# The sample's projections leave PSUM by two ScalarE copies and are summed in SBUF; the gated values are scaled in the order of their groups

## The chip, the core and the metric

The kernel runs on one core of one Trainium2 chip. The metric is the device time of one execution in microseconds (us). A core has five engines that run side by side, each through its own queue in order: PE (TensorE: matrix products and transposes; its weight loads are shown apart, as PEld), DVE (VectorE), ACT (ScalarE), POOL (GpSimd) and SP (SyncE, which here starts transfers). PE writes its results to PSUM, which this kernel handles as eight banks of 128 x 512 numbers; everything else lies in SBUF. An instruction that needs another engine's result, or a buffer that another engine still reads, waits at the head of its queue, and everything behind it waits too.

## What is computed

The program runs two layers of an encoder over 512 prompt positions and 32 sample positions, 544 together, of width 1024. A layer has a mixer, a cross-attention into 256 memory rows, and a feed-forward part with a short convolution. The change lies in the mixer, which in the reference is:

```
h = rmsnorm(x, w['norm_mix_g'])
z = h @ w['w_in']
q, k, v, u, gv = jnp.split(z, [c1, c2, c3, c4], axis=-1)
o = diff_attention(q, k_all, v_all, pos, k_pos, lam)
u = jax.nn.gelu(u)
gv = rmsnorm(jax.nn.gelu(gv).reshape(B, S, GM_GROUPS, GM_CH), w['gm_norm_g'])
g_out = spatial_gate(u, gv, w['gm_w_s'], w['gm_b'])
x = x + jnp.concatenate([o, g_out], axis=-1) @ w['w_out']
```

q, k and v feed a differential attention with four heads: two softmax maps per head, the second subtracted with a learned factor. u and gv feed a gate with four groups of 128 channels: each group of gv is normalized, multiplied by a lower triangular 128 x 128 matrix over chunks of 128 positions, and multiplied into u. Prompt and sample share the weights; the sample also attends to cached keys and values.

## The kernel before

**Precision.** A float32 operand is split into a high part and a low rest, and a product takes three matmuls: high by high, high by low, low by high. Weights arrive by DMA as `raw`, ACT casts the high part (L192) and DVE subtracts to get the rest (L193); both go to slots named `hl`, of which there are eight. These splits run ahead of their use in the gaps of ACT and DVE.

**Projections by position.** `proj_tm` (L374) makes a slice of 256 columns of k and q, of v or of gv. The prompt takes four groups of 24 matmuls (`tm_group`, L370 to L372) into two banks `pr`. The sample takes 16 matmuls (L387) into one bank `prs`: `xsm` holds the high and the low part of the sample's rows side by side, so that rows 0 to 31 of the bank hold the high part's product and rows 32 to 63 the low part's. `sum_s` (L409) adds the two: ACT copies rows 32 to 63 to a scratch (`zs1`, which the trace names `skq` after its tile), and DVE adds rows 0 to 31 of the bank and the scratch into `zs`, in a tile that the trace names `zvs`. It runs eight times a layer: four times for k and q, twice for v, twice for gv.

**Attention.** For a head, `kq_T` transposes k and q (`ptr`, and `ptrs` for the sample). `do_attn` then goes over four blocks of 128 queries: scores (L639, L641) into two banks `pS`; the maximum on DVE (L597), the exponential on ACT (L598), the two maps joined on DVE (L603); the result transposed on PE (L649, `paT`), copied by ACT (L651), and multiplied with v (L654, `po`); `take_o` copies it and sums its squares on ACT. After four blocks a chain of small DVE operations finds the scales (`subnorm`), ACT applies them (L624), PE transposes (L660, `poT`), and ACT and DVE put the head's output into `og`. `do_attn_sample` does the same for the 32 sample queries (`pSs`, `paTs`, `pos`, and `posT` for two heads together).

**Gate.** `do_gv` (L721) projects gv for two groups, applies the gelu in three DVE passes and two ACT passes, sums the squares of its eight 128 x 128 pieces (four chunks of two groups), finds the scales by a chain of small DVE operations (L744, then `rsq`: L247 to L254), and scales the eight pieces on ACT (L747). `do_us` projects u (L353 into `pua` and `pub`, 96 matmuls for a column of 128). `do_gate` (L754) multiplies four pieces of one group with its matrix (L763, `pg`) and then those of the other; DVE reads the result (L765) and multiplies it into u (L792). Then w_out is projected from `og` (L353, `pwoa` and `pwob`).

**What sets the order.** The layer's code fixes the heads, but the order in each engine's queue is made at build time by a scheduler that works with its own estimate of durations. PSUM comes from three pools: four banks "R" (`pr`, `prs`, `ptr`, `ptrs`, `pg`, `pgs`, `pua`, `pub`), two "S" (`pS`, `pSs`), two "B" (`paT`, `po`, `poT`, `paTs`, `pos`, `posT`). A bank goes to its next user when its last reader is done. So a small edit moves instructions far from its place.

Of the kernel before, what the change touches and what calls it, by code (L numbers as in the profile page):

```python
# [13 lines left out]
ALU = mybir.AluOpType  # L14
# [22 lines left out]
def encoder_step(ctx: ExitStack, tc: tile.TileContext, a, o):  # L37
    nc = tc.nc
    vec, act, pool, pe, sp = nc.vector, nc.scalar, nc.gpsimd, nc.tensor, nc.sync
# [10 lines left out]
    def psS(name):  # L50
        return pp.tile([128, 512], F32, tag="S", bufs=2, name=name)
# [6 lines left out]
    def G(tag, shape, name, dt=F32):  # L58
        return gp.tile(shape, dt, tag=tag, bufs=GB[tag], name=name)
# [6 lines left out]
    def tiny(shape, name, dt=F32):  # L66
        return tp.tile(shape, dt, tag="y_" + name, bufs=1 if name in ONCE else 2, name=name)
# [159 lines left out]
    def pop(tag, n=2):  # L227

        for i in state.pop("done", ()):
            state["held"] -= cost(i)  # L230
        i = state["popped"]
        prefetch()
        res = []
        for j in range(i, i + n):
            assert items[j][0] == tag, (items[j], tag)
            res.append(wt.pop(j))
        state["popped"] = i + n
        state["done"] = range(i, i + n)
        return res


    def rsq(v, p, n, name, eng=vec):

        y, h, t = (tp.tile([128, n], F32, tag=f"{name}_{v}", bufs=2 if v == "y" else 1, name=name + v)
                   for v in "yht")
        yy, hh, tt = y[0:p, 0:n], h[0:p, 0:n], t[0:p, 0:n]
        eng.tensor_scalar(out=yy.bitcast(I32), in0=v.bitcast(I32), scalar1=-0.5, scalar2=1597463007.0,  # L247
                          op0=ALU.mult, op1=ALU.add)
        eng.tensor_scalar(out=hh, in0=v, scalar1=-0.5, scalar2=None, op0=ALU.mult)
        for _ in range(3):  # L250
            eng.tensor_tensor(out=tt, in0=yy, in1=yy, op=ALU.mult)
            eng.tensor_tensor(out=tt, in0=tt, in1=hh, op=ALU.mult)
            if eng is vec:
                vec.scalar_tensor_tensor(out=yy, in0=tt, scalar=1.5, in1=yy, op0=ALU.add, op1=ALU.mult)  # L254
            else:
                eng.tensor_scalar(out=tt, in0=tt, scalar1=1.5, scalar2=None, op0=ALU.add)
                eng.tensor_tensor(out=yy, in0=tt, in1=yy, op=ALU.mult)
        return y
# [5 lines left out]
    def gelu2(z, t):  # L264

        act.activation(out=t, in_=z, func=AF.Square, scale=math.sqrt(0.044715))
        vec.scalar_tensor_tensor(out=t, in0=t, scalar=1.0, in1=z, op0=ALU.add, op1=ALU.mult)
        act.activation(out=t, in_=t, func=AF.Tanh, scale=GC)
        vec.scalar_tensor_tensor(out=z, in0=t, scalar=1.0, in1=z, op0=ALU.add, op1=ALU.mult)
# [32 lines left out]
    def psR2(name, n=0):  # L302
        f = psS if n % 3 == 2 else psR
        return [f(name + "a"), f(name + "b")]
# [69 lines left out]
    def proj_tm(w2):  # L374
        pr, pv = [], []
        for t in range(4):
            t0 = 128 * t
            if t % 2 == 0:
                ps = psR("pr").rearrange("p (t c) -> p t c", t=2)
            pr.append(ps[:, t % 2])  # L380
            tm_group(pr[t], lambda k: hx[:, k, 0, t0:t0 + 128], lambda k: hx[:, k, 1, t0:t0 + 128], w2)
            if t % 2:
                pv.append(ps)
        ps = psR("prs")
        for k in range(8):
            for part in range(2):
                pe.matmul(out=ps[0:64, 0:256], lhsT=xsm[:, k], rhs=w2[k // 4][part][:, k % 4],  # L387
                          start=(k == 0 and part == 0), stop=(k == 7 and part == 1))
        return pr, pv, ps
# [15 lines left out]
    def small_z(kind):  # L405
        small[kind].reverse()
        return small[kind][0]

    def sum_s(ps, name):  # L409
        zt = small["zs1"]  # L410
        zs = small_z("vs" if name == "vs" else "zs")
        act.copy(zt, ps[32:64, 0:256])
        vec.tensor_tensor(out=zs[0:32], in0=ps[0:32, 0:256], in1=zt, op=ALU.add)  # L413
        return zs


# [101 lines left out]
    def do_kq(l, h, ve):  # L518
        c = LC[l]
        pr, pv, prs = proj_tm(pop(f"kq{h}"))  # L520
        z = G("zr", [128, 4, 256], "z")
        sq = G("t4", [128, 4, 256], "sq")
        for i in range(2):
            act.copy(z[:, 2 * i:2 * i + 2], pv[i])
            act.activation(out=sq[:, 2 * i:2 * i + 2], in_=pv[i], func=AF.Square)
        zs = sum_s(prs, "zs")
        sqs = small["zs1"]
        act.activation(out=sqs, in_=zs[0:32], func=AF.Square)
        ss = tiny([128, 20], "ss")
        pool.memset(ss[:, 16:20], 1.0)  # L530
        vec.tensor_reduce(out=ss[:, 0:16], in_=sq.rearrange("p t (m d) -> p (t m) d", d=64), axis=AX, op=ALU.add)
        vec.tensor_reduce(out=ss[0:32, 16:20], in_=sqs.rearrange("p (m d) -> p m d", d=64), axis=AX, op=ALU.add)
        s5 = ss.rearrange("p (t m) -> p t m", m=4)
        vec.scalar_tensor_tensor(out=s5, in0=s5, scalar=1.0 / 64, in1=ve.unsqueeze(2).to_broadcast([128, 5, 4]),
                                 op0=ALU.mult, op1=ALU.add)
        rs = rsq(ss, 128, 20, "rk")
        norm_rope(z, 128, 4, None, rs[:, 0:16], c, 0)
        norm_rope(zs[0:32].unsqueeze(1), 32, 1, None, rs[0:32, 16:20], c, 4)
        sp.dma_start(out=o["dkp"][l, 0, :, h].rearrange("(t p) m d -> p t (m d)", p=128), in_=z[:, :, 0:128])
        sp.dma_start(out=o["dks"][l, 0, :, h].rearrange("p m d -> p (m d)"), in_=zs[0:32, 0:128])  # L540
        return z, zs
# [179 lines left out]
    def do_gv(l, j, r):  # L721
        c = LC[l]
        pr, _, prs = proj_tm(pop(f"gv{j}"))
        z = G("zr", [128, 4, 256], "gz")
        t1 = G("t4", [128, 4, 256], "gt")
        for t in range(4):
            act.activation(out=z[:, t], in_=pr[t], func=AF.Copy,
                           scale=r[:, t:t + 1])
        zs = sum_s(prs, "gzs")
        vec.tensor_scalar(out=zs[0:32], in0=zs[0:32], scalar1=r[0:32, 4:5], scalar2=None, op0=ALU.mult)  # L730
        t1s = small["zs1"]
        ss = tiny([128, 10], "gss")
        pool.memset(ss[:, 8:10], 1.0)
        gelu2(z, t1)
        gelu2(zs[0:32], t1s)
        z8 = z.rearrange("p t (g c) -> p (t g) c", c=128)
        zs2 = zs[0:32].rearrange("p (g c) -> p g c", c=128)
        for b in range(8):
            act.activation(out=t1[:, b // 2, 128 * (b % 2):128 * (b % 2) + 128], in_=z8[:, b], func=AF.Square,
                           accum_out=ss[:, b:b + 1])  # L740
        for b in range(2):
            act.activation(out=t1s[:, 128 * b:128 * b + 128], in_=zs2[:, b], func=AF.Square,
                           accum_out=ss[0:32, 8 + b:9 + b])
        vec.tensor_scalar(out=ss, in0=ss, scalar1=1.0 / 128, scalar2=4 * EPS, op0=ALU.mult, op1=ALU.add)  # L744
        rs = rsq(ss, 128, 10, "rg")
        for b in range(8):
            act.activation(out=z8[:, b], in_=z8[:, b], func=AF.Copy, scale=rs[:, b:b + 1])  # L747
        vec.tensor_tensor(out=zs2, in0=zs2, in1=rs[0:32, 8:10].unsqueeze(2).to_broadcast([32, 2, 128]), op=ALU.mult)
        vec.tensor_tensor(out=t1s.rearrange("p (g c) -> p g c", c=128), in0=zs2,
                          in1=c["gmg"][0:32].unsqueeze(1).to_broadcast([32, 2, 128]), op=ALU.mult)  # L750
        sp.dma_start(out=o["gvs"][l, 0, :, 2 * j:2 * j + 2].rearrange("p g c -> p (g c)"), in_=t1s)
        return z, zs
# [428 lines left out]
    for t in range(4):  # L1181
        for hk in range(2):
            ps = (psB if hk else psS)("pxin")
# [4 lines left out]
        if t == 0:  # L1188
            ps = psS("pxis")
# [11 lines left out]
    for l in range(DEPTH):  # L1201
# [25 lines left out]
        do_attn_sample_end(l, 0, og, st)  # L1227
        zk[3] = do_kq(l, 3, ve)
        vns[0] = do_gv(l, 0, r)
        kqs[3] = kq_T(l, 3, *zk[3])  # L1230
        do_attn(l, 3, kqs[3], vv[3], og)
        do_attn_sample(l, 3, kqs[3], vv[3], st)
        og += [G("kq", [128, 2, T], "gg", F32R) for _ in range(4)]
        us[0] = do_us(l, 0, rbc)
        vns[1] = do_gv(l, 1, r)
        do_gated(l, 0, us[0], vns[0], ws, og)
        us[1] = do_us(l, 1, rbc)
# [6 lines left out]
        for j in range(4):  # L1244
            w2 = pop(f"wout{j}")
            for i in range(2):
                ps = psR2("pwo", 2 * j + i + 2)
# [18 lines left out]
        for j in range(4):  # L1266
            w2 = pop(f"wo{j}")
            for i in range(2):
                ps = psR2("pwc")
# [54 lines left out]
```

## Time and profile before

| what | value |
|---|---|
| median of 3 runs | 1645.56 us (1643.87 to 1646.12) |
| the profiled execution's own time | 1646.09 us |
| its span in the trace | 1643.6 us |
| granted clock of TensorE, mean | 0.999 of full speed |
| PE busy | 98% of the span |
| DVE, ACT, POOL busy | 70%, 47%, 33% |

The profiled execution lies 0.53 us above the median, and its span is 2.5 us shorter than its time, which is what lies around the program. In the page's 40 slices PE is busy for 90% or more in all but the first and the last. The mixers, which the change touches, run from about 20 to 220 us and from 830 to 1030 us.

### The profile page before, as it was taken

How to read it: one execution, taken by the hardware profiler on the slowest of the kernel's cores; microseconds unless marked ns; L12 is line 12 of the kernel's file. 1: busy time of each engine (PE TensorE's matmuls, PEld its weight loads, DVE VectorE, ACT ScalarE, POOL GpSimd, SP SyncE). 2: the span in 40 equal slices, each digit the busy share in tenths (PEclk: the TensorE clock that was granted, in tenths of full speed). 3: DMA queues.
4: the chain of work that ended last, by engine and by line, in shares of the span. 5: the costliest groups of instructions: out<-in, count | busy, mean ns of one | idle time of the engine just before them, and what ended most of it. 6: DMA issues, size and time to landing. Idle time of an engine off the chain costs nothing.

```text
span 1643.6 us, 33008 instructions
## 1 busy us (share of the span) xinstructions
PE 1618.4 (98%) x12897; PEld 1590.4 (97%) x12897; DVE 1149.6 (70%) x2454; ACT 778.0 (47%) x1625; POOL 538.3 (33%) x910
## 2 busy tenths in 40 slices
PE   8999999999999999999999999999999999999998
PEld 8999999899999999999999999999999999999998
DVE  6779765555477777877778777555555878778774
ACT  6567644544344334343446586545543433343331
POOL 2010042222244554543320100422232555555440
PEclk9999999999999999999999999999999999999999
DMA  7322224332322332323342222243422323323322
GB/s 212 91 82 88 79 91 131 113 122 93 89 72 80 92 105 82 95 80 100 111 123 63 81 70 86 91 129 110 136 84 78 90 81 93 94 81 94 91 81 82
DMA packets 217649, 158.06 MB, mean 96 GB/s; under 512 B 8430, under 2 KB 216182, under 8 KB 217494
## 3 DMA queue, kind: packets, MB, share of 16 engines
q1 hardware_dynamic: 217158, 155.69, 31.4%
q8 instruction: 101, 1.65, 0.4%
q14 instruction: 54, 0.44, 0.1%
q10 hardware_dynamic: 336, 0.27, 0.1%
HBM read 144.83 MB, written 11.10 MB: 95 GB/s over the span
## 4 chain that ended last, share of the span: by engine, by line
PE 92%; ACT 2%; DVE 2%; POOL 2%; DMA 1%; issue 1%; SPq 1%; DVEq 0%; ACTq 0%; POOLq 0%
PE pfga L353 8%; PE pfgb L353 8%; PE pfua L353 8%; PE pfub L353 8%; PE p7a L1084 6%; PE pr L370 3%; PE pr L372 3%; PE pr L371 3%; PE p7c L1084 3%; PE pwoa L353 3%; PE pwca L353 3%; PE pqb L353 3%; PE pwob L353 3%; PE pqa L353 3%; PE pwcb L353 3%; PE pm L372 2%
## 5 line engine op out<-in xcount | busy, mean ns | idle before, releaser
L193 DVE TENSOR_TENSOR hl<-raw,hl 128x1024 fp32r<-128x1024 f32 x216 | 278.3, 1289 | 93.7 <-ACT hl L192 89.6
L192 ACT CAST hl<-raw 128x1024 fp32r<-128x1024 f32 x216 | 226.6, 1049 | 159.4 <-PE pm L371 36.6
L353 PE MATMUL pfub<-hx,hl 128*128 128x272 f32 x1056 | 264.5, 287 | 0.0
L353 PE MATMUL pfga<-hx,hl 128*128 128x272 f32 x1056 | 264.5, 287 | 0.0
L353 PE MATMUL pfua<-hx,hl 128*128 128x272 f32 x1056 | 264.4, 287 | 0.0
L353 PE MATMUL pfgb<-hx,hl 128*128 128x272 f32 x1056 | 264.4, 287 | 0.0
L353 PEld LDWEIGHTS pfga<-hx,hl 128*128 128x128 f32 x1056 | 198.5, 188 | 0.0
L353 PEld LDWEIGHTS pfgb<-hx,hl 128*128 128x128 f32 x1056 | 198.4, 188 | 0.0
L353 PEld LDWEIGHTS pfua<-hx,hl 128*128 128x128 f32 x1056 | 198.0, 188 | 0.0
L353 PEld LDWEIGHTS pfub<-hx,hl 128*128 128x128 f32 x1056 | 197.9, 188 | 0.0
L370 PE MATMUL pr<-hl,hx 128*128 128x256 f32 x512 | 145.5, 285 | 1.1 <-DVE zvs L413 0.7
L371 PE MATMUL pr<-hl,hx 128*128 128x256 f32 x512 | 145.8, 285 | 0.0
L372 PE MATMUL pr<-hl,hx 128*128 128x256 f32 x512 | 145.3, 285 | 0.0
L1084 PE MATMUL p7a<-at,hl 128*128 128x272 f32 x864 | 121.8, 287 | 0.0
L1084 PEld LDWEIGHTS p7a<-at,hl 128*128 128x128 f32 x864 | 113.3, 188 | 0.0
L210 ACT CAST hl<-S 128x384 fp32r<-128x384 f32 x96 | 48.4, 512 | 111.1 <-POOL S L200 41.6
L370 PEld LDWEIGHTS pr<-hl,hx 128*128 128x128 f32 x512 | 98.2, 192 | 2.1 <-DVE zvs L413 1.2
L372 PEld LDWEIGHTS pr<-hl,hx 128*128 128x128 f32 x512 | 96.8, 189 | 0.6 <-DVE hx L1177 0.3
L371 PEld LDWEIGHTS pr<-hl,hx 128*128 128x128 f32 x512 | 96.8, 189 | 0.3
L210 ACT CAST hl<-raw 128x384 fp32r<-128x384 f32 x72 | 36.6, 511 | 108.5 <-PE pfub L353 60.9
L353 PE MATMUL pwca<-co,hl 128*128 128x272 f32 x384 | 87.5, 289 | 0.0
L353 PE MATMUL pwcb<-co,hl 128*128 128x272 f32 x384 | 87.1, 288 | 0.0
(400 smaller groups left out, 4202.3 us busy)
## 6 DMA issues: line engine op xcount, KB each, us to landing
raw<-in_w_up_dram SPq DMA_DIRECT2D x88, 512.0 KB
raw<-in_w_down_dram SPq DMA_DIRECT2D x48, 384.0 KB
raw<-in_w_in_dram SPq DMA_DIRECT2D x24, 512.0 KB
raw<-in_w_in_dram SPq DMA_DIRECT2D x32, 256.0 KB
raw<-in_w_out_dram SPq DMA_DIRECT2D x32, 256.0 KB
raw<-in_wq_c_dram SPq DMA_DIRECT2D x16, 512.0 KB
raw<-in_wk_c_dram SPq DMA_DIRECT2D x16, 512.0 KB
raw<-in_wv_c_dram SPq DMA_DIRECT2D x16, 512.0 KB
```

The lines of the kernel that those rows point to most:

```text
L192: act.copy(hi, src)
L193: vec.tensor_tensor(out=lo, in0=src, in1=f32(hi), op=ALU.subtract)
L210: act.copy(hl[:, 0], src)
L353: pe.matmul(out=ps[0 if n0 == 0 else 1][:, 0:nn], lhsT=hl[wpart][:, kk, col * 128:col * 128 + 128], rhs=mv[:, n0:n0 + nn], start=first and ...
L370: pe.matmul(out=out, lhsT=lh(k), rhs=hl[0][:, k % 4], start=(k == 0), stop=False)
L371: pe.matmul(out=out, lhsT=lh(k), rhs=hl[1][:, k % 4], start=False, stop=False)
L372: pe.matmul(out=out, lhsT=ll(k), rhs=hl[0][:, k % 4], start=False, stop=(k == k8 - 1))
L1084: pe.matmul(out=ps, lhsT=w[:, wpart, k], rhs=mv[:, part], start=fresh and k == 0 and wpart + part == 0, stop=k == PART - 1 and wpart == 1, ...
```

## The change

Two edits, and what the scheduler makes of them.

```
     act.copy(zt, ps[32:64, 0:256])
-    vec.tensor_tensor(out=zs[0:32], in0=ps[0:32, 0:256], in1=zt, op=ALU.add)
+    act.copy(zs[0:32], ps[0:32, 0:256])
+    vec.tensor_tensor(out=zs[0:32], in0=zs[0:32], in1=zt, op=ALU.add)
     return zs
...
     rs = rsq(ss, 128, 10, "rg")
-    for b in range(8):
+    for b in (0, 2, 4, 6, 1, 3, 5, 7):
         act.activation(out=z8[:, b], in_=z8[:, b], func=AF.Copy, scale=rs[:, b:b + 1])
```

In `sum_s` ACT copies both halves out of the bank, and DVE adds them in SBUF. The bank's last reader is then ACT's second copy, no longer DVE's addition. ACT has 16 instructions more in all; the other engines have as many as before. In `do_gv` the pieces with even numbers belong to the first group, those with odd numbers to the second; the loop now scales the four of the first group, then the four of the second. Lines behind L412 are numbered one higher after the change.

The order of PE's queue is the same up to the first head's attention and in the feed-forward parts; in between, in both layers' mixers alike, it is made anew. Two places follow.

The first is head 0's last block of queries (the `po` of four matmuls), where head 2's k and q are transposed (`ptr`, `ptrs`) and a new projection begins (`pr`). PE's queue before:

```order
L387 MATMUL prs<-hl,xsm 64x256 x9
L654 MATMUL po<-vr,e 128x128 x3
L553 MATMUL ptr<-ident,z 128x128 x8
L568 MATMUL ptrs<-ident,ck 128x128 x2
L649 MATMUL paT<-ident,e 128x128 x4
L570 MATMUL ptrs<-ident,zvs 128x128 x2
L654 MATMUL po<-vr,e 128x128 x4
L370 MATMUL pr<-hl,hx 128x256
```

PE's queue there after:

```order
L387 MATMUL prs<-hl,xsm 64x256 x3
L554 MATMUL ptr<-ident,z 128x128 x8
L569 MATMUL ptrs<-ident,ck 128x128 x2
L571 MATMUL ptrs<-ident,zvs 128x128
L650 MATMUL paT<-ident,e 128x128 x4
L571 MATMUL ptrs<-ident,zvs 128x128
L370 MATMUL pr<-hl,hx 128x256
```

The next projection now begins ahead of the four `po`; 31 of its matmuls stand between the last `ptrs` and the first `po`. The same place in ACT's queue, before:

```order
L412 COPY skq<-prs 32x256
L610 COPY sot<-po 128x128
L611 ACTIVATE junk,sso<-po 128x128
L557 CAST kT<-ptr 64x512
L676 ACTIVATE es,mxs<-pSs,mxs 128x288
L560 ACTIVATE qT<-ptr 64x512
L651 COPY e<-paT 128x512
```

And after:

```order
L612 ACTIVATE junk,sso<-po 128x128
L677 ACTIVATE es,mxs<-pSs,mxs 128x288
L192 CAST hl<-raw 128x1024
L412 COPY skq<-prs 32x256
L413 COPY zvs<-prs 32x256
L558 CAST kT<-ptr 64x512
L561 ACTIVATE qT<-ptr 64x512
L652 COPY e<-paT 128x512
```

The two copies out of `prs` stand next to each other, behind a weight split and the sample's exponential.

The second place is head 3's attention, the last of a layer, beside the projection of u for the second two groups (`pua`, `pub`). PE's queue before:

```order
L763 MATMUL pg<-wsT,gz 128x128 x6
L773 MATMUL pgs<-wsT,zvs 128x32 x2
L649 MATMUL paT<-ident,e 128x128
L654 MATMUL po<-vr,e 128x128
L353 MATMUL pua<-hx,hl 128x272 x24
L649 MATMUL paT<-ident,e 128x128 x2
L639 MATMUL pS<-kT,qT 128x512
L641 MATMUL pS<-kT,ql 128x512
L353 MATMUL pub<-hx,hl 128x272 x6
```

PE's queue there after, from the last two of the 96 matmuls of `pua` and `pub`:

```order
L353 MATMUL pua<-hx,hl 128x272
L353 MATMUL pub<-hx,hl 128x272
L661 MATMUL poT<-ident,sot 128x128
L684 MATMUL paTs<-es 128x32 x2
L684 MATMUL paTs<-es 32x32
L661 MATMUL poT<-ident,sot 128x128 x3
L690 MATMUL pos<-cv,aTs 32x128 x2
L691 MATMUL pos<-zvs,aTs 32x128
```

All 96 stand ahead of head 2's `poT` and the transposes (`paT`) of head 3's first block, where before those transposes stood in front of and among them. On DVE, at the join of head 3's second block (`e`, 128 x 256), the queue before was:

```order
L685 COPY aTs<-paTs 128x64
L686 COPY aTs<-paTs 32x32
L600 RECIPROCAL ri<-sm 128x1
L601 TENSOR_SCALAR ri<-sm,ri,nlam_275 128x1
L603 SCALAR_TENSOR_TENSOR e<-e,ri 128x256
L663 SCALAR_TENSOR_TENSOR og<-poT,sub_262,og 128x512
```

And after:

```order
L193 TENSOR_TENSOR hl<-raw,hl 128x1024
L252 TENSOR_TENSOR rgt<-rgt,rgh 128x10
L601 RECIPROCAL ri<-sm 128x1
L644 MEMSET pS 64x64
L254 SCALAR_TENSOR_TENSOR rgy<-rgt,rgy 128x10
L644 MEMSET pS 64x64
L664 SCALAR_TENSOR_TENSOR og<-poT,sub_262,og 128x512
L602 TENSOR_SCALAR ri<-sm,ri,nlam_275 128x1
L598 TENSOR_REDUCE mx<-pS 128x1 x2
L251 TENSOR_TENSOR rgt<-rgy 128x10
L267 SCALAR_TENSOR_TENSOR ut<-ut,u 128x544
L604 SCALAR_TENSOR_TENSOR e<-e,ri 128x256
```

The join of that block now stands behind a weight split, head 2's output, the maxima of the third block and a gelu pass.

## Rows read from the trace of the kernel before

**Rows 1.** The page: busy us, share of the span, count, by engine.

```profile
PE 1618.4 (98%) x12897; PEld 1590.4 (97%) x12897; DVE 1149.6 (70%) x2454; ACT 778.0 (47%) x1625; POOL 538.3 (33%) x910
```

**Rows 2.** Windows: length; busy us (count) of PE, PEld, DVE, ACT, POOL; clock; DMA.

```profile
60.00:100.00 40.00, 38.54 (x317) 37.21 (x316) 34.60 (x118) 24.83 (x70) 4.23 (x12) 1.00 0.25 75
...
220.00:270.00 50.00, 50.00 (x406) 49.97 (x406) 29.51 (x46) 28.15 (x48) 19.78 (x24) 1.00 0.30 96
...
140.00:150.00 10.00, 9.89 (x74) 9.64 (x75) 9.31 (x30) 9.87 (x44) 1.60 (x4) 1.00 0.32 99
177.70:197.50 19.80, 19.39 (x153) 18.92 (x151) 18.51 (x52) 15.12 (x56) 1.71 (x5) 1.00 0.26 80
```

**Rows 3.** What PE waited for, whole span: total us, times, longest us.

```profile
PE po L654 <- ACT e L651: 4.2, 6, 1.5
PE pg L763 <- ACT gz L747: 1.8, 2, 0.9
PE pua L353 <- DVE zvs L413: 1.5, 2, 0.7
...
PE pr L370 <- DVE zvs L413: 0.7, 2, 0.4
```

**Rows 4.** Readers of the bank `prs`: duration ns least/median/most, first and last start.

```profile
L412 ACT COPY skq<-prs x16: 363/364/368, 26.2 to 984.6; 32x256 f32<-32x256 f32 x16
L413 DVE TENSOR_TENSOR zvs<-prs,skq x16: 395/405/412, 26.7 to 987.6; 32x256 f32<-32x256 f32 x16
```

**Rows 5.** Timeline behind head 0's first transposes: start, duration, instruction [idle before].

```profile
45.98 0.37 ACT L412 COPY skq<-prs 32x256 f32<-32x256 f32 x1 [0.39 <-ACT hl L192]
...
47.23 0.39 PE L370 MATMUL pr<-hl,hx 128*128 128x256 f32 x1 [0.34 <-DVE zvs L413]
```

**Rows 6.** Timeline at head 0's last block.

```profile
79.05 2.35 DVE L193 TENSOR_TENSOR hl<-raw,hl 128x1024 fp32r<-128x1024 f32 x2
79.43 0.37 ACT L412 COPY skq<-prs 32x256 f32<-32x256 f32 x1
...
81.68 0.58 ACT L651 COPY e<-paT 128x512 f32<-128x512 f32 x1
...
82.31 0.94 PE L654 MATMUL po<-vr,e 128*128 128x128 f32 x6 [1.46 <-ACT e L651]
```

**Rows 7.** Timeline at the first projection of u.

```profile
138.66 0.49 PE L654 MATMUL po<-vr,e 128*128 128x128 f32 x2 [0.27 <-ACT e L651]
...
140.11 1.64 PE L353 MATMUL pua<-hx,hl 128*128 128x272 f32 x11 [0.74 <-DVE zvs L413]
```

**Rows 8.** Timeline at head 3 and the second gate; x counts records merged into one row.

```profile
174.31 1.60 PE L763 MATMUL pg<-wsT,gz 128*128 128x128 f32 x12
...
177.03 3.27 PE L353 MATMUL pua<-hx,hl 128*128 128x272 f32 x24
...
197.56 2.44 ACT L747 ACTIVATE gz<-gz,rgy 128x128 f32<-128x128 f32 x8
197.70 0.16 DVE L620 SCALAR_TENSOR_TENSOR s<-sso,s 128x4 f32<-128x4 f32 x1 [0.26 <-ACT junk L611]
198.01 0.78 PE L763 MATMUL pg<-wsT,gz 128*128 128x128 f32 x4 [0.91 <-ACT gz L747]
...
200.53 0.69 ACT L624 ACTIVATE sot<-sot,roy 128x128 f32<-128x128 f32 x2 [0.53 <-DVE roy L254]
```

**Rows 9.** Groups of DVE, 173 to 203 us: count | busy us, mean ns | idle.

```profile
L193 DVE TENSOR_TENSOR hl<-raw,hl 128x1024 fp32r<-128x1024 f32 x4 | 4.9, 1220 | 0.6 <-ACT hl L192 0.6
...
L267 DVE SCALAR_TENSOR_TENSOR ut<-ut,u 128x544 f32<-128x544 f32 x2 | 1.5, 726 | 0.2 <-ACT ut L266 0.2
...
L597 DVE TENSOR_REDUCE mx<-pS 128x1 f32<-128x384 f32 x2 | 1.0, 524 | 0.0
...
L787 DVE TENSOR_TENSOR u<-pub,rbc 128x272 f32<-128x272 f32 x2 | 0.9, 427 | 0.0
...
L748 DVE TENSOR_TENSOR zvs<-zvs,rgy 32x256 f32<-32x256 f32 x1 | 0.4, 411 | 0.0
```

## The prediction, made before the changed kernel was run

> **What bounds the kernel now.** I read the busy times first: TensorE is busy 98% of the span, so little is left to win, and a loss has to come from new gaps in its row [rows 1]. The windows say where gaps can be. In the feed-forward stretch PE is busy 50.00 of 50 us; from 60 to 100 us, in the mixer, 38.54 of 40 [rows 2]. All that the change moves lies in the mixers, and the two mixers show the same waits. So I price one mixer and double it.
>
> The waits of PE name the gaps: `po` behind ACT's copy of the transposes, 4.2 us in 6 waits, the longest 1.5; the gate behind ACT's scaling, 1.8 in 2; `pua` and `pr` behind the sample's sum on DVE, 1.5 and 0.7 in 2 each [rows 3]. These the change can take away. The last views are the busy times of DVE and ACT where PE is nearly full: from 177.7 to 197.5 us DVE is busy 18.51 of 19.80 us, and from 140 to 150 ACT is busy 9.87 of 10 [rows 2]. What the new order puts behind these engines is what can newly stall PE.
>
> **The edits themselves.** The new copies are 16, each like L412 at 0.364 us: 5.8 us of ACT [rows 4]. ACT is busy 47% [rows 1], so most go into gaps; where ACT is full, each delays what stands behind it by 0.36, which I put into the terms below. The addition stays on DVE: with an operand in PSUM it takes 0.405 us [rows 4], and a 32 x 256 operation wholly in SBUF takes 0.411 [rows 9]. I take no gain there. [...] The order of the pieces lets the first four matmuls start after four of eight scalings; eight take 2.44 us [rows 8], so four take 1.22.
>
> **Gains, for one mixer.** First, behind head 0's first transposes: the bank was freed by DVE's sum, which stood behind a split, and `pr` waited 0.34 us. ACT's copy ended at 45.98 + 0.37 = 46.35, and a second behind it at some 46.7, before `pr` starts at 47.23 [rows 5]. The wait goes: 0.35.
>
> Second, head 0's last block. The four `po` waited 1.46 us for ACT's copy of the transposes, which ran from 81.68 to 82.26 [rows 6]. Now 31 matmuls of `pr` stand ahead of them; at the pitch of the projection of u, (3.27 - 0.28)/24 = 0.125 us [rows 8], they are 3.9 us of cover. They need the bank, whose last reader is now the second copy, behind the sample's exponential and a split of 1.05 us or so. So the gap may shrink and not vanish: between 0.5 and 1.46, taken 1.0.
>
> Third, the first projection of u waited 0.27 us at a `po` just before, and 0.74 us for the sum on DVE [rows 7]. Behind ACT's copies the bank comes free earlier, but the next bank still hangs on ACT's copies out of `ptrs`. I take 0.3 (between 0 and 1.0). The gains sum to 1.65 (0.85 to 2.8).
>
> **Losses, for one mixer.** The new order runs all 96 matmuls of u for the last two groups before head 3's transposes. Before, these transposes lay among them, so each softmax had a dozen matmuls or more to hide behind. Now I compare two queues from the end of the last `prs`.
>
> PE has, to the transposes of head 3's second block: the gate matmuls 1.9 (eight of them in sixteen records, at 1.60 for twelve [rows 8], with drains in between left out), 96 x 0.125 = 12.0 for u, and 24 short ones (`pgs`, `pS`, `poT`, `paTs`, `pos`, `posT`, one `paT` and `po`). Four `po` take 0.94 [rows 6], so 0.17 each with overlap is an estimate: 4.15. Sum 18.05.
>
> DVE has, from the first gate read to the join of that block, 58 instructions:
> - 3 splits of 1.22: 3.66;
> - 10 passes of 128 x 512 or 544 (gelu, gating, gate reads, head 2's output), at 0.73: 7.3, and one of 128 x 1024, at 1.2: an estimate from the pass of half its width;
> - 4 reads of u, at 0.427: 1.71;
> - 4 maxima, two at 0.52 and two narrower ones estimated at 0.42: 1.89, and 2 joins estimated together at 0.8;
> - 4 of 32 x 256, three at 0.41 and one at 0.33 by estimate: 1.56;
> - 30 small ones at 0.16 to 0.17: 5.1.
>
> The prices are from [rows 9], the small one from [rows 8]. The sum is 23.2. Neighbours overlap: two splits of 1.22 take 2.35 [rows 6, 9], so 0.09 less; with 0.07 for each of the 58 the queue takes 19.1 us if never idle. It starts some 0.9 us behind PE, after the first four gate matmuls. So the join comes 19.1 + 0.9 - 18.05 = 1.95 us after PE wants it. But DVE is not without gaps: in the fullest stretch before it needed 19.80 us for 18.51 of work [rows 2]. With that factor the queue takes 20.4, and PE waits 3.25. A second reckoning agrees with the lower value: the copies of `paTs` on DVE can't start before PE has made them, near 15.3 us; 4.7 us of DVE follow to the join, against 2.2 us of PE. I take 3.2; bounds 1.9 and 4.7, the upper with two more waits such as those of 0.91 and 0.53 [rows 8].
>
> At the second gate, `pg` waited 0.91 us [rows 8]. Now four scalings are enough, and PE has some matmuls of its own there; 0.5 is left, a gain of 0.4. At the end of head 3 the chain from the sum of squares to the scaling takes 200.53 - 197.70 = 2.83 us [rows 8]. In the new order it has a split of 1.2 among it and, around it, the take of the last block (0.45) and the first scaling (0.33): 4.9 us against 27 matmuls of w_out, 3.4. That leaves 1.4 (0 to 1.6). The sample's `pos` of that head now stands right behind it instead of after 27 matmuls: 0.3 (0 to 0.5).
>
> Losses: 3.2 - 0.4 + 1.4 + 0.3 = 4.5 (1.5 to 6.4).
>
> **Sum.** For one mixer 4.5 - 1.65 = +2.85, with ends 1.5 - 2.8 = -1.3 and 6.4 - 0.85 = +5.5. Twice: +5.7 (-2.6 to +11). On the profiled execution 1646.09 + 5.7 = 1651.8; against the median, 0.53 lower, 1651.3 (1643.0 to 1656.6).
>
> **The rivals.** About 0.2%, 3.3 us, is what a measurement of this kernel can tell from no change: faster means below 1642.3, slower above 1648.8.
>
> *The cover holds.* DVE does not run 19 us behind a PE that needs 18: a split or two fall into gaps before the stretch, as the slots `hl` allow. It decides at two splits: without 2.4 us of the 19.1, the queue, 16.7 + 0.9, ends before PE's 18.05, and the terms of head 3 vanish. Then the gains stand alone, 1.65 + 0.4 a mixer, 4.1 in all: 1641.5, down to 1638.2 if each gain has its full size (2.8 + 0.9). For it: the waits to be removed are in the record, each with DVE's sum or ACT's copy named [rows 3]. Against it: the stretch before already kept DVE at 18.51 of 19.80 [rows 2]. [...] Chance 0.17.
>
> *Gain and loss cancel.* The stall at the join is at its lower bound or the chain at the end is hidden: losses of 1.5 to 2.5 against gains of 1.65. That gives within 2 us of 1645.6. Chance 0.25.
>
> *The bank is no earlier.* ACT's two copies stand behind a split and the sample's exponential, and the bank comes free as late as by DVE. It decides when ACT runs more than 0.5 us behind where it ran; from 140 to 150 us it had no gap left [rows 2]. The gains vanish and the loss stays: +9.0, 1654.6. Chance 0.06.
>
> **How the numbers follow.** The forecast, the loss at head 3 outweighing the gains, 1648.8 to 1655 with 1651.3 in the middle, has 0.52. Faster: the first rival, 0.17. Same: the second, 0.25. Slower: forecast and third, 0.58. The range reaches down to the middle of the first rival, 1641.5, and up to the sum's upper end, 1656.5; outside are half of that rival and a part of the third's upper side, some 0.13 together, and about 0.05 for what I have not thought of.
>
> **What would show it.** In the profile after: `po` at head 0's last block without its wait of 1.46 and `pua` and `pr` no longer waiting for the sum; at head 3, waits of PE for DVE's join (through `paT`) or the copies of `paTs`, 2 to 4.7 us in each mixer; at the end of the mixer `poT` waiting some 1.4 for the scaling; the gate's wait down to about 0.5; DVE without a gap over 19 us from the first gate read. The feed-forward and cross-attention windows stay as they are. I am wrong if no wait of head 3 exceeds 1 us, or if the first waits stay.

## The result, and the profile after

The change costs time: 1653.2 us (four runs, 1652.52 to 1655.16) against 1644.71 us for the kernel before on the same chip (1643.58 to 1646.12). The ratio is 1.0054, with an interval of 1.0042 to 1.0066, so +8.5 us where +5.7 was forecast. The profiled execution took 1655.16 us, 2.0 above its own median, with a span of 1653.4 and a mean granted clock of 0.996 (before: 0.999).

The busy times by engine on the page after, answering [rows 1]:

```profile
PE 1626.2 (98%) x12897; PEld 1595.3 (96%) x12897; DVE 1149.6 (70%) x2454; ACT 781.6 (47%) x1641; POOL 545.2 (33%) x910
```

DVE has not changed at all, and ACT has its 16 copies (+3.6 us busy). PE has the same instructions, yet 7.8 us more busy time: the same matmuls ran slower somewhere. That is the first sign of something the forecast did not have. Cut at the first matmul of each part, the two traces differ as follows.

```
us                                         before    after
start to the first projection              10.76     10.27
layer 1, to the cross-attention's output  375.33    380.80   +5.5
layer 1, from there to the feed-forward    54.57     54.60
layer 1, feed-forward                     385.40    385.20
layer 2, to the cross-attention's output  368.94    371.94   +3.0
layer 2, from there to the feed-forward    54.59     54.59
layer 2, feed-forward to the end          394.05    396.04   +2.0
```

The last +2.0 has the same instructions in the same order on both sides, 1.3 of it behind the last matmul. It is about what the profiled run lies above its median, and I leave it out. The loss lies in the stretches with the mixers, 5.5 us in the first layer and 3.0 in the second.

What PE waited for, over the whole span, in after (total us, times, longest us), answering [rows 3]:

```profile
PE poT L661 <- ACT sot L625: 2.8, 4, 1.2
PE posT L701 <- ACT junk L612: 1.8, 2, 0.9
...
PE pr L370 <- ACT zvs L413: 1.4, 2, 0.7
...
PE paT L650 <- DVE e L604: 0.8, 1, 0.8
PE po L655 <- ACT e L652: 0.7, 2, 0.4
...
PE paT L650 <- DVE rgt L252: 0.6, 1, 0.6
```

All four waits that the forecast wanted gone are gone or smaller: `pua` and `pg` no longer appear, `po` fell from 4.2 to 0.7, and `pr` now waits at another place (head 0's last block). New are `poT`, `posT` and `paT`, all at head 3; the first `poT` there is still head 2's. Head 3 of the first layer in the timeline after (start, duration, instruction, idle before and who ended it); the last of the 96 matmuls of u starts at 182.49:

```profile
183.09 0.33 PE L661 MATMUL poT<-ident,sot 128*128 128x128 f32 x1 [0.31 <-ACT sot L625]
...
187.34 0.31 PE L701 MATMUL posT<-ident,sot 32*128 32x32 f32 x2 [0.91 <-ACT junk L612]
...
188.26 0.80 PE L655 MATMUL po<-vr,e 128*128 128x128 f32 x2 [0.35 <-ACT e L652]
189.68 0.69 PE L650 MATMUL paT<-ident,e 128*128 128x128 f32 x2 [0.62 <-DVE rgt L252]
...
210.53 0.33 PE L661 MATMUL poT<-ident,sot 128*128 128x128 f32 x1 [1.25 <-ACT sot L625]
```

From 183 to 190 us PE does only short work and stops four times, 2.19 us in all; at the end of the head it stops once more, 1.25. In the second layer the four are 0.31, 0.90, 0.35 and 0.84, and the stop at the end is 0.88. Before, PE's only named wait from 177 to 204 us was the gate's 0.91 [rows 8]. DVE's part in it was forecast closely. Its first gate read and the join of the second block in after:

```profile
169.50 0.74 DVE L766 SCALAR_TENSOR_TENSOR s<-pg,cols,gmb 128x512 f32<-128x512 f32 x1
...
188.96 0.48 DVE L604 SCALAR_TENSOR_TENSOR e<-e,ri 128x256 f32<-128x256 f32 x1
```

That is 19.94 us from the start of the one to the end of the other, where 19.1 to 20.4 was forecast; it began 1.7 behind PE's first gate matmul (167.82), where 0.9 was taken. That end, 189.44, is what the `paT` at 189.68 waited for; the row names the small L252 beside it.

What was not forecast is the clock. Windows of after (length; busy us and count of PE, PEld, DVE, ACT, POOL; granted clock; DMA):

```profile
182.00:190.00 8.00, 5.66 (x34) 3.81 (x32) 7.75 (x27) 6.71 (x26) 0.88 (x2) 0.88 0.40 131
190.00:196.00 6.00, 6.00 (x29) 5.33 (x28) 4.89 (x16) 5.81 (x22) 0.41 (x3) 0.59 0.06 12
196.00:208.00 12.00, 12.00 (x99) 11.89 (x99) 7.38 (x23) 4.91 (x15) 0.60 (x3) 1.00 0.23 67
...
212.00:216.00 4.00, 4.00 (x20) 3.20 (x19) 2.25 (x12) 1.12 (x4) 0.00 (x0) 0.57 0.35 135
...
1004.00:1010.00 6.00, 5.49 (x33) 5.01 (x34) 5.25 (x19) 5.98 (x23) 0.25 (x2) 0.72 0.01 2
...
1022.00:1026.00 4.00, 3.12 (x24) 2.25 (x23) 1.54 (x10) 1.98 (x6) 0.00 (x0) 1.00 0.54 168
```

Behind the gaps of head 3 the granted clock is 0.59 over six us, behind the gap of 1.25 it is 0.57 over four, and in the second layer 0.72: in windows of one us it reads 0.50 in each from 189 to 194, from 213 to 215 and from 1004 to 1007, and nowhere in these stretches less. PE is busy for the whole of 190 to 196 and does 29 matmuls of mixed sizes; from 196 to 208, with the clock at 1.00, it does 99 in twice the time. Behind the second layer's gap of 0.88, in the last window, the clock stayed at 1.00. In the kernel before, all these windows read 1.00; the second one, and those behind its waits of 1.46 and 0.91:

```profile
190.00:196.00 6.00, 6.00 (x51) 6.00 (x51) 5.73 (x21) 4.01 (x10) 0.81 (x3) 1.00 0.44 139
```

```profile
82.00:84.00 2.00, 1.69 (x14) 1.69 (x15) 1.81 (x6) 1.92 (x7) 0.46 (x1) 1.00 0.94 309
...
198.00:200.00 2.00, 1.99 (x16) 1.99 (x17) 1.50 (x11) 2.00 (x7) 0.31 (x1) 1.00 0.85 263
```

### The profile page after: what moved, and what is told of

Its sections match the earlier page's. It is cut to its first block, busy times and chain, and to the rows that moved or that the text cites. A ratio compares the mean times of both kernels' runs of the same rounds, so it can differ in the third digit from the quotient of the medians.

```text
span 1653.4 us, 33046 instructions
## 1 busy us (share of the span) xinstructions
PE 1626.2 (98%) x12897; PEld 1595.3 (96%) x12897; DVE 1149.6 (70%) x2454; ACT 781.6 (47%) x1641; POOL 545.2 (33%) x910
## 4 chain that ended last, share of the span: by engine, by line
PE 91%; POOL 2%; DVE 2%; ACT 2%; issue 1%; DMA 1%; DVEq 0%; ACTq 0%; POOLq 0%; SPq 0%
PE pfga L353 8%; PE pfgb L353 8%; PE pfua L353 7%; PE pfub L353 7%; PE p7a L1085 6%; PE pr L370 4%; PE pr L372 4%; PE pr L371 4%; PE p7c L1085 3%; PE pwca L353 3%; PE pqb L353 3%; PE pwoa L353 3%; PE pqa L353 3%; PE pwcb L353 3%; PE pwob L353 3%; PE prs L387 2%
## 5 line engine op out<-in xcount | busy, mean ns | idle before, releaser
L200 POOL TENSOR_TENSOR S<-raw 128x384 f32<-128x384 f32 x48 | 61.1, 1273 | 79.5 <-DMA raw<-in_w_down_dram 62.6
```

Source lines behind the costliest of these rows:

```text
L200: pool.tensor_tensor(out=t, in0=in0, in1=in1, op=op)
```

## The experiments

Two questions were to be told apart. Does the loss come from the **edits** (the second copy, the scalings) or from the **order** that the scheduler made of them? And is it idle time of PE alone, or idle time and the **clock** behind it?

In the kernels "in a written order" the queue of every engine is fixed to a recorded one, by edges between neighbours in the queue, so that an edit can't move anything else:

```
for first, then in zip(queue, queue[1:]):
    tc.add_manual_dep(then, first.name, mybir.DependencyInfo(
        mybir.DependencyClass.NoSync, mybir.DependencyReason.DATA), reason="written order")
```

The second copy stands right behind the first one there. Ratios are against the kernel before, run beside each kernel on the same chip.

**One edit at a time, the scheduler's own order.** First the edit of `sum_s` alone:

> The kernel before with the new sum_s alone; the scheduler orders it anew (its order is that of the changed kernel but for the rows around the second gate). Theory A (the loss is the new order, made by the sum): about as slow as the changed kernel, 1650 to 1655 us, with PE's gaps at head 3 and the lower clock behind them. Rival B (the scaling loop made the order, or its matmuls cost): within 3 us of 1645.

Measured: 1659.41 us, ratio 1.0081 (1.0068 to 1.0095), worse than both edits together. The scheduler makes nearly the order of after from this edit (70 of PE's 12897 instructions stand elsewhere), and the wait of `poT` is longer in it. What PE waited for:

```profile
PE poT L661 <- ACT sot L625: 4.3, 4, 2.0
```

So the sum's edit is what turns the order over. The five runs of this one kernel also differ with the clock: 1655.04 us at a mean granted clock of 0.996, 1657.62 at 0.994, and 1659.41 to 1661.7 at 0.992. Then the edit of the loop alone:

> The kernel before with the new order of the scalings alone; the scheduler leaves the order of before but for a few rows around the second gate. Theory A: PE's wait of 0.9 us for the scaling goes in each mixer, nothing else moves: 1642.5 to 1644.5 us. Rival B (the loop carries the loss): above 1648 us.

Measured: 1646.16, ratio 1.0010 (1.0001 to 1.0018): no gain, and the wait that was to go has stayed. Timeline of this kernel at the second gate:

```profile
196.40 2.44 ACT L747 ACTIVATE gz<-gz,rgy 128x128 f32<-128x128 f32 x8
...
196.86 1.65 PE L763 MATMUL pg<-wsT,gz 128*128 128x128 f32 x10 [0.91 <-ACT gz L747]
```

The matmul starts 0.46 us after the first scaling starts, as in [rows 8] (197.56 and 198.01), where one scaling takes 0.39. So it waits for one scaling, not for four or eight, and the order among the eight can't shorten that.

**The edits in the order of before.** The sum alone:

> The new sum_s alone, every queue held to the written order of the kernel before. By the traces so far the wait behind head 0's first transposes goes (0.5 us a mixer), the wait at the first u shrinks by 0.4, and two waits for ACT grow by 0.25 each; the second wait at the gate of the run with both edits (0.8) should not be there, since the scalings keep their order. Theory T: 1644 to 1646 us. Rival C (16 copies on ACT cost by themselves): 1647 to 1650 us.

Measured: 1644.44, ratio 0.9993 (0.9984 to 1.0003). The 16 copies cost nothing that can be measured, and they gain nothing by themselves. What PE waited for in this kernel:

```profile
PE po L656 <- ACT e L653: 5.1, 6, 1.7
...
PE pub L353 <- ACT skq L578: 0.8, 2, 0.4
```

The waits for the sum (`pr` and `pua`) are gone, 1.5 + 0.7 of [rows 3]. But `po` behind ACT's copy went up from 4.2 to 5.1, which fits a second copy that delays ACT (not tested by itself), and `pub` now waits 0.8 for another of ACT's copies. Both edits:

> Both edits, but every engine's queue is held to the written order of the kernel before; each new copy of ACT stands right behind the old one, and nothing else moves. Theory A (the order alone loses, the edits gain): PE's waits for the sum, 0.34 and 0.74 us, and for the scaling, 0.9 us, go or shrink in each mixer: 1640.5 to 1643.5 us, faster than before. Rival C (16 copies more on ACT delay what stands behind them and cost by themselves): 1646 to 1651 us.

Measured: 1648.96, ratio 1.0021 (1.0012 to 1.0030). In before's order PE asks early for one piece of each group, and the first piece of the second group is now scaled fifth. Timeline, and the window behind:

```profile
196.88 0.49 PE L765 MATMUL pg<-wsT,gz 128*128 128x128 f32 x2 [0.91 <-ACT gz L749]
198.04 0.49 PE L765 MATMUL pg<-wsT,gz 128*128 128x128 f32 x2 [0.67 <-ACT gz L749]
...
198.00:202.00 4.00, 3.96 (x21) 3.96 (x22) 1.13 (x7) 2.14 (x7) 0.31 (x1) 0.61 0.24 89
```

A second gap of 0.67 us close behind the first, and the clock reads 0.61 over the next four us. In before, the gap of 0.91 stood alone and the clock stayed at 1.00. But the pair of gaps does not always bring the fall: the second layer has the same two, and the clock behind them stayed at 1.00.

```profile
1008.33 0.49 PE L765 MATMUL pg<-wsT,gz 128*128 128x128 f32 x2 [0.91 <-ACT gz L749]
1009.49 0.49 PE L765 MATMUL pg<-wsT,gz 128*128 128x128 f32 x2 [0.67 <-ACT gz L749]
```

```profile
1010.00:1012.00 2.00, 2.00 (x18) 2.00 (x18) 1.14 (x7) 0.59 (x3) 0.31 (x1) 1.00 0.12 44
```

Nor is it the same in every execution: the eleven runs go from 1646.19 us at a mean clock of 1.000 to 1650.59 at 0.997.

**The order of after, without the edits.**

> Neither edit, but every engine's queue is held to the written order of the changed kernel, with the 16 added copies of ACT left out. Theory A: the gaps at head 3 and the lower clock are there without any edit, and the waits for the sum come back: 1653 to 1658 us. Rival C (the copies on ACT cost): 1644 to 1648 us.

Measured: 1657.69, ratio 1.0083 (1.0070 to 1.0096). What PE waited for:

```profile
PE pr L370 <- DVE zvs L413: 4.0, 4, 1.7
PE poT L660 <- ACT sot L624: 3.3, 4, 1.8
PE pua L353 <- DVE zvs L413: 2.4, 2, 1.2
```

This trace is of an execution of 1662.82 us, 5.1 above the median, at a clock of 0.993 where the other four had 0.997. The order alone loses 0.83%, some 13.6 us of the 1645, and inside it the edits win back 0.29% (1.0083 to 1.0054), some 4.8 us: there `pr` waits 1.4 instead of 4.0 and `pua` not at all. No `pg` wait appears here either, though the scalings stand as in before: the order took that wait away, not the loop.

**Where in the order the loss sits.** Both kernels run after's order to a cut and before's order behind it, in both mixers. The first is cut behind head 0's last block and has the sum's edit alone:

> The new sum_s alone, in a written order: in each mixer the changed kernel's order up to head 0's last block, the order of before behind it. Theory T: keeps the first two gains (0.5 and 0.8 us a mixer) and none of the loss at head 3: 1642 to 1644 us. Rival E (the loss begins ahead of head 3): above 1646 us.

Measured: 1643.01, ratio 0.9988 (0.9979 to 0.9996): faster than both kernels, by a little. What PE waited for:

```profile
PE pg L765 <- ACT gz L749: 1.8, 2, 0.9
PE po L656 <- ACT e L653: 1.8, 4, 0.5
```

`po` is at 1.8 instead of 5.1 in the kernel that kept before's order throughout, so what the new order does at head 0 takes waits away; in time the two are not told apart (0.9988 and 0.9993). The second, too, has the sum's edit alone; it is cut just ahead of the first projection of u:

> As the run before, but the changed kernel's order up to just ahead of the first projection of u, the order of before behind it. Theory T: keeps the first two gains, no loss at head 3, but the join of the two orders may cost a wait of some 1 us for head 1's transposes: 1641.5 to 1645.5 us. Rival E: above 1647 us, with gaps at head 3.

Measured: 1650.82, ratio 1.0034 (1.0021 to 1.0046). The seam of the two orders made a gap of its own, so this run says nothing on where after's loss sits; the gaps of head 3 are gone in it. It does show the clock behind one long gap. The wait, and windows in and behind it:

```profile
PE poT L662 <- ACT sot L626: 4.8, 2, 2.4
...
131.00:134.00 3.00, 0.59 (x7) 0.55 (x6) 1.89 (x12) 1.00 (x4) 0.00 (x0) 1.00 0.00 0
135.00:137.00 2.00, 2.00 (x10) 2.00 (x10) 1.09 (x7) 2.00 (x7) 0.19 (x1) 0.50 0.00 0
```

After 2.41 us without work, PE is busy for two full us at a clock of 0.50 and starts 10 matmuls, of 256 and 384 columns; just before the gap, with 1.00 in the window from 129 to 131, those of 256 start 0.12 us apart.

**The clock by itself.** The computation and the order of after, with 19 transposes more per mixer that nobody reads, put into PE's gaps ahead of `poT`, `posT`, `po` and `paT`. They do no useful work and only keep PE busy:

```
+        fills = [pe.transpose(pt[:, 0:128], ident, ident).ins.name for _ in range(8)] if h == 3 else []
...
+        for place, n in (("posT", 5), ("po", 2), ("paT", 4)):
+            AHEAD[gap[place]] = [pe.transpose(gap["bank"][:, 0:128], ident, ident).ins.name for _ in range(n)]
```

In a first try three of the four groups wrote to the free columns of a bank that other engines still read:

> The changed kernel in its own order, with 19 transposes added in each mixer whose results nobody reads, placed where PE stands idle at head 3 (5 ahead of posT, 2 ahead of the first po, 4 ahead of the second block's transposes, 8 ahead of the last poT). Theory T (most of the loss is the clock that falls behind those gaps): the waits of the others stay, the granted clock stays at 1.00 there, and the time falls by 3 to 6 us, to 1647.5 to 1650.5 us. Rival G (the gaps themselves are the loss, the clock follows without cost): 1652 to 1656 us, since the added work shortens no wait.

Measured: 1654.59, ratio 1.0056 (1.0043 to 1.0069), no different from after. Those three groups waited themselves, the fills in front of `posT` among them (they are all at L630, and carry the bank's name); only the eight ahead of the last `poT` ran in their gap. What PE waited for, and windows:

```profile
PE pos L630 <- ACT junk L613: 1.8, 2, 0.9
...
190.00:196.00 6.00, 5.26 (x27) 4.34 (x28) 4.23 (x17) 5.37 (x21) 0.19 (x1) 0.72 0.01 2
...
212.00:216.00 4.00, 3.91 (x29) 3.04 (x29) 2.54 (x14) 1.44 (x5) 0.00 (x0) 1.00 0.52 171
```

Where the gap was filled the clock behind it is 1.00 (0.57 in after); where it was not, it fell again (0.72). In the second try all of them write to a bank that nobody reads at that time:

> As the run that filled the gaps, but the transposes ahead of posT, po and paT (5, 2, 4) write to a bank that nobody reads any more, so that they can run while PE waits (there the first three groups waited themselves, and only the eight ahead of poT ran in their gap; behind those the clock stayed at 1.00). The results are not read; nothing of the computation is left out. Theory T (the clock is most of the loss): the granted clock stays at 1.00 behind head 3 and behind poT, and the time falls to 1647 to 1650 us though no wait of others is shortened. Rival G (the gaps themselves are the loss): 1652 to 1656 us.

Measured: 1648.86, ratio 1.0025 (1.0015 to 1.0036). Windows:

```profile
182.00:190.00 8.00, 6.66 (x46) 4.90 (x45) 7.74 (x25) 7.03 (x26) 0.88 (x2) 1.00 0.40 131
190.00:196.00 6.00, 5.74 (x41) 4.87 (x42) 5.49 (x22) 6.00 (x22) 0.66 (x3) 1.00 0.07 14
...
212.00:216.00 4.00, 3.91 (x29) 3.69 (x30) 3.01 (x16) 1.21 (x5) 0.00 (x0) 1.00 0.32 119
...
1004.00:1010.00 6.00, 6.00 (x51) 5.89 (x50) 5.88 (x17) 4.75 (x16) 0.47 (x2) 1.00 0.02 5
```

The clock is back at 1.00 in all four places, and the kernel is 4.3 us faster than after (1653.2 to 1648.86; the two intervals don't overlap) with 38 instructions more. The same eight gate matmuls behind the gaps, in after and in this kernel:

```profile
192.96 1.91 PE L764 MATMUL pg<-wsT,gz 128*128 128x128 f32 x8
```

```profile
192.47 1.11 PE L776 MATMUL pg<-wsT,gz 128*128 128x128 f32 x8
```

But not all of the 4.3 is the clock's. Matched instruction by instruction, the filled kernel is 0.4 us behind after up to head 3 of the first layer (183.52 against 183.09), 1.9 ahead behind it (214.01 against 215.94), and goes from 2.7 to 3.2 ahead at head 3 of the second: 2.3 and 0.5 us, won where after's clock was low, net of 0.6 that the last `poT`, waiting for the scaling, took back. The two profiled executions differ by more, and 2.0 us of that lies in the feed-forward parts, where the clock is 1.00 in both. In the first layer, after and then this kernel:

```profile
445.67:830.87 385.20, 384.40 (x3083) 384.00 (x3082) 295.82 (x498) 151.13 (x232) 184.62 (x245) 1.00 0.31 92
```

```profile
443.65:828.14 384.49, 384.49 (x3084) 384.00 (x3082) 296.77 (x498) 151.12 (x232) 184.85 (x245) 1.00 0.32 92
```

The first try has this too (384.59 there), though its clock fell; what shortens the feed-forward is open. So of the 8.5 us about 2.8 is shown to be the clock, and about 5.7 is left: the idle time and the short steps at head 3, less the gains.

**Who sets the waits of head 3.** Three kernels shorten what stands ahead of the join in DVE's queue, all in after's order otherwise. Below, `+` and `-` are moves in that queue. In the first, a split of 1.2 us (with its cast on ACT) goes behind the join; in the second, the join (with the small step L602 before it) goes ahead of the third block's masks and maxima; the third does both.

```
-L193 TENSOR_TENSOR hl<-raw,hl          (first and third kernel)
...
+L604 SCALAR_TENSOR_TENSOR e<-e,ri      (second and third kernel)
 L644 MEMSET pS
...
 L664 SCALAR_TENSOR_TENSOR og<-poT
 L598 TENSOR_REDUCE mx<-pS x2
...
-L604 SCALAR_TENSOR_TENSOR e<-e,ri      (second and third kernel)
+L193 TENSOR_TENSOR hl<-raw,hl          (first and third kernel)
```

> The changed kernel in its own order, but in each mixer one weight split (ACT's cast of 1.05 us and DVE's subtraction of 1.22) is moved from ahead of the join of head 3's second block to behind it. Theory T (the stretch at head 3 is set by the queues of DVE and ACT): PE's waits there, 2.5 us in the first mixer by the rows, fall by 1.2 or more, and with shorter gaps the clock falls less: 1647 to 1651 us. Rival R (the gaps are set by chains of results, not by what is queued): the waits stay, 1652 to 1655 us.

Measured: 1655.6, ratio 1.0062 (1.0049 to 1.0076).

> The changed kernel in its own order, but on DVE the join of head 3's second block (with the small step before it) stands right behind its reciprocal, ahead of the masks and maxima of the third block, head 2's output and a gelu pass. Theory S (the join waits in DVE's queue behind masks that wait for PE's own scores): PE's wait for the join, 0.6 us in the first mixer and 1.0 in the run with one split later, goes; the wait of 0.9 for ACT ahead of posT stays, and the clock still falls, if for less: 1650 to 1653 us. Rival Q (the amount of DVE work sets the stretch): the waits move and the sum stays, 1653 to 1656 us.

Measured: 1654.83, ratio 1.0060 (1.0047 to 1.0072).

> As the run before, and the weight split of ACT and DVE behind the join too, which alone had shortened PE's wait for ACT (0.9 to 0.2 us) and lengthened that for the join (0.6 to 1.1). Theory S: both waits are short now, the gaps at head 3 come to 1.0 to 1.3 us in place of 2.2, the clock stays at 1.00 there: 1647 to 1650 us. Rival Q: 1652 to 1656 us.

Measured: 1653.05, ratio 1.0050 (1.0036 to 1.0064). None is told apart from after. The waits in the first mixer, in the order of PE's queue, from the four timelines:

```
us                     poT    posT   paT    po     paT    sum
after                  0.31   0.91   -      0.35   0.62   2.19
a split later          0.32   0.23   0.40   0.35   1.07   2.37
the join first         0.31   0.92   0.48   0.35   0.62   2.68
both                   0.32   0.24   0.39   0.35   0.90   2.20
```

Each edit does at its own place what it should, and the sum stays. The row of `paT` behind the join, in the first kernel, then in the second with the join ahead of it:

```profile
190.65 0.41 PE L651 MATMUL paT<-ident,e 128*128 128x128 f32 x2 [1.07 <-DVE e L605]
```

```profile
185.70 0.48 DVE L605 SCALAR_TENSOR_TENSOR e<-e,ri 128x256 f32<-128x256 f32 x1
...
189.44 0.69 PE L651 MATMUL paT<-ident,e 128*128 128x128 f32 x2 [0.62 <-ACT junk L613]
```

In the second kernel the join starts 3.3 us earlier than in after (185.70 against 188.96), and `paT` waits the same 0.62, now for ACT to finish reading the bank that `po` left. In the first, DVE itself has to wait, at the mask of the next scores, for PE:

```profile
187.23 0.11 DVE L645 MEMSET pS<- 64x64 f32 x1 [0.87 <-PE pS L643]
```

So no one of these moves shortens this stretch. `poT`, `paTs`, `pos`, `posT`, `paT`, `po` and `paT` go one after the other through the two "B" banks, each needs ACT or DVE to read the one before, and PE has nothing else to do there, since the 96 matmuls of u are spent. Putting some of them back between these steps, by hand, was not tried.

## Why the prediction was right, and where it was not

**Right: the sign, the order as its cause, and the place.** Slower, and by the order: before's order with the sum's edit costs nothing (0.9993), after's order without any edit costs 0.83%. The new waits stand at head 3, where all 96 matmuls of u now run ahead of the transposes. That their missing cover makes these waits fits the traces; it was not shown by a run, as none put them back. By its own test, a wait of head 3 over 1 us, the forecast holds through one wait only, the 1.25 at the head's end in the first layer; the four at the blocks are each below 1, and in the second layer none is above 0.90. The rival in which the bank comes no earlier is out, since the waits of `pua` and `po` went. The one in which the cover holds is out too: the queue of DVE took 19.94 us. The one in which gain and loss cancel is out by the time.

**Missing: a term for the clock.** The forecast took a microsecond of idle PE as a microsecond of loss, and named no other cost. About 2.8 of the 8.5 us came from the lower clock behind the gaps (0.59, 0.57 and 0.72 in the windows above), as the filled gaps show. The trace of before held no instance of it: its waits of 1.46 and 0.91 stand alone, with 1.00 behind them. What the sum of +5.7 should be compared with is what is left without the clock: 5.5 - 2.3 = 3.2 us in the first layer and 3.0 - 0.5 = 2.5 in the second, where 2.85 a mixer was forecast. That part came out nearly right, but in part by luck, since gains and losses were both too small.

**The losses.** The wait at the end of head 3 was right in the first layer (1.25 against 1.4) and too high in the second (0.88). At head 3's blocks 3.2 was taken as one wait for the join. From the first gate matmul behind the last `prs`, 167.82, to the second block's `paT` at 189.68 PE took 21.9 us, 3.8 over the 18.05 of its own work by the forecast's reckoning, but only 2.19 of that is named waits and 0.62 of it is at the join, where 2 us or more was to show. The other 1.6 is the short matmuls, 5.8 us without the waits where 4.15 was an estimate (the gate, 1.8, and u, 12.1, took what was forecast); the last of them ran at the lower clock, by the window above (0.88). So the size came out and the reason only in half. The forecast has one queue, DVE's, running 19 us behind a PE that needs 18; the three kernels above shorten or reorder that queue, and the waits add up to no less. The `pos` wait of 0.3 is not in the trace; the `posT` wait of 0.91, which was not foreseen, is.

**The gains.** They were too small, 2.05 us a mixer. The wait behind head 0's first transposes went (0.35 forecast, 0.34 gone). At head 0's last block the wait fell from 1.46 to 0.70, so 0.76 of the 1.0, and ACT's second copy is what now ends last, as the forecast said; timeline of after:

```profile
80.24 0.36 ACT L413 COPY zvs<-prs 32x256 f32<-32x256 f32 x1
...
80.65 0.39 PE L370 MATMUL pr<-hl,hx 128*128 128x256 f32 x1 [0.70 <-ACT zvs L413]
```

At the first projection of u 0.3 was taken, with 1.0 as the upper end, and 1.0 came: both waits of [rows 7], 0.27 and 0.74, are gone. The next bank does not hold PE up there. At the second gate 0.4 was taken and 0.91 came, and the step behind it was wrong: "after four of eight scalings" misread a row in which eight are merged, while the wait ended with the first. In total 0.34 + 0.76 + 1.0 + 0.91 = 3.0 us of named waits a mixer instead of 2.05.

**The whole of a mixer.** In the second layer the two traces can be added up from each PE start to the next, by the tile of the next:

```
us         po      pua,pub  pg,pgs  poT    posT   paT    pS,pSs,paTs,pos  the rest
before     11.91   25.61    5.80    1.93   0.72   4.57   16.78            356.21
after      10.27   24.75    4.31    3.59   1.87   5.83   17.86            358.06
           -1.64   -0.86    -1.49   +1.66  +1.15  +1.26  +1.08            +1.85
```

Gains of 4.0 and losses of 7.0 leave +3.0, where the forecast had 2.05 and 4.9 with +2.85. The forecast had half of the gains and 70% of the losses, and the misses cancelled. The losses hold the clock's 0.5, and 0.7 of the rest stands at `pmk` in the cross-attention, whose waits vary from 0.3 to 0.9 us in all among the kernels with before's order. In the first layer the same sum gives +5.5.

**The addition.** No gain was taken for its operand in SBUF, and there is none: 405 ns in the median in after, 405 in [rows 4].

```profile
L414 DVE TENSOR_TENSOR zvs<-zvs,skq x16: 395/405/414, 26.5 to 987.0; 32x256 f32<-32x256 f32 x16
```

The two copies freed the bank earlier, and the waits for it went at `pua` and at head 0's first `pr`, but DVE kept every instruction: 2454 on both pages.

**Open.** The two layers' mixers show nearly the same waits, but filling the gaps brought 2.3 us in the first and 0.5 in the second. The windows go with that: if each is reckoned as a mixture of 1.00 and 0.50, the clock was low for some 10 us of the first mixer (0.88 over 8 us, 0.59 over 6, 0.57 over 4) and for some 3 of the second (0.72 over 6). Why it was low for a shorter time there is not known, and 1.5 us of the 4.3 that the filling brought is not the clock's by these traces and has no cause named.

## What to carry to other kernels

Before pricing a small edit under a scheduler, ask what order comes out, and measure order and edit apart by writing the queues down: here the sum's edit was free in the old order, and the new order cost 0.8%. Where PE is nearly full, look for runs of short steps that pass through the same few banks, and keep some independent matmuls back for them; here shortening the queue that one wait names only handed the wait to the next, and keeping matmuls back is a proposal that no run tried. And when several gaps of PE move close together, add a price for the clock behind them to the gaps themselves: here a third of the loss.

## What the runs showed of the hardware

The granted clock fell behind gaps that single waits of much the same size had not caused: 1.46 us and 0.91 us alone left it at 1.00 in before, while 2.19 us in four pieces within 7 us, 0.91 and 0.67 close together, and 2.41 in one piece were followed by 0.59, 0.61 and 0.50 in the windows behind. The gaps alone do not tell, though. The gap of 1.25 us at 210.5 was followed by 0.57, some 20 us behind the others; the same 0.91 and 0.67 left the clock at 1.00 in the second layer of that kernel; and executions of one kernel differed by 0.003 to 0.004 in their mean clock and by 4 to 7 us in time. What decides it is open. With the clock at 0.50 (0.52 in the last us) eight gate matmuls took 1.91 us; at 1.00, with the gaps filled, they took 1.11. Transposes that nobody reads, run in the gaps, kept the clock at 1.00 and made the kernel 4.3 us faster with more work in it, 2.8 of it where the clock had been low.
